# Slack for steps off the recurrence in an order planner, in a two-layer encoder kernel

## The chip, the cores and the metric

One Trainium2 chip, one of its cores. The metric is the device time of one execution of the whole kernel in microseconds (us), lower is better. A core has a matrix engine (PE, with its weight loads PEld), a vector engine (DVE), an activation engine (ACT), GpSimd (POOL) and a queue of transfers (SP); each runs its own list of instructions strictly in the order in which the program gives them.

## The reference

Two layers over 2048 frames of 1024 channels, all in float32:

```python
c_act = silu(c)
for i in range(2):
    shift, scale, gate = split(c_act @ ada_w[i] + ada_b[i])
    h = rmsnorm(x, norm_g[i]) * (1 + scale) + shift
    out = rglru_block(h, ...) if i == 0 else gated_deltanet_block(h, ...)
    x = x + gate * out
return rmsnorm(x, final_g)

# rglru_block: xb, zg = h @ in_w; causal conv of width 4 on xb; two gates, each a
#   product of 8 blocks of 128x128; a linear scan over time; y * silu(zg) @ out_w
# gated_deltanet_block, 8 heads of 128: q, k, v, z = h @ in_w; causal conv of width 4 and
#   silu on q, k, v; q and k to unit length; then by head, chunk after chunk,
#   step: v_new = u_c - w_c @ state;  o_c = q_c @ state + attn_c @ v_new
#         state = state * e_c + k_c^T @ v_new
#   o * rsqrt(mean(o^2) + eps) * onorm_g * silu(z) @ out_w
```

## The kernel before

A float32 product is made as three matmuls of a rounded type: each operand is split into a high part `hi` (a cast, on ACT) and a low part `lo` (`raw - hi`, on GpSimd for weights), and hi*hi, hi*lo, lo*hi are summed. The weights come in panels of 128 columns (512 KB): `panels_thread` loads one into a buffer `raw`, casts it to `whi` (L640) and subtracts to `wlo` (L646). There are two `raw` buffers, and the rows of the adaLN weights (`araw`, L402) and the output weights (`oraw`, L892) use the same two. `products` (L664) then issues 24 matmuls of 128x512 for one panel and one half of the tokens, into a PSUM bank `mm`. The 2048 frames are taken in two halves of 1024 (`u`), each in two parts of 512 (`i`): layer 1 is `in1` 0 and 1, then its output product `out1`, layer 2 `in2` 0 and 1, then `out2`.

In layer 2, `conv2_thread` copies the bank to `xe` on ACT (L726), which frees the bank, and convolves it on DVE (`xf`, L714), to a `kt`, `qt` or `vt` tile. By head and part, off the state's recurrence:

- `key_thread` loads the row of decays to all partitions (`ec`, L1117), masks it on GpSimd (L1119), takes its exponential on ACT (L1123) and makes the block matrix `ac`.
- `norm_q_thread` turns q by 32x32 blocks on DVE (`tokens_of`, `tb`), writes it to DRAM (`q_d`, L1223), reads it back as `pq` (L1197) and sums its squares on ACT (`junkq`, L1203); GpSimd makes `rq` of it.
- `value_thread` does the same with v (`v_d`, `vn`, L1235), and scales it on ACT (L1239).
- `outputs_thread` makes the scale `ro` on GpSimd (L1482), applies it on ACT (`oo`, L1487), turns it and writes `o_d`.
- `inverses_thread` and `levels_thread` invert the block (long runs of small DVE operations, `ttmp` and `tblk`, L1285 and L1288).

`recurrence_thread` then runs the chunks one after the other: `pp` on PE from the state (L1405), `zt` on DVE (L1414), `py` on PE (L1422), `yt` on ACT (L1428), `pS` on PE (L1434), `state` on DVE (L1447). The matmuls of the next heads' panels are issued between these steps.

Nothing of this order is written by hand. Each `..._thread` is a Python generator, and the class `Weave` is a planner that runs while the program is built: a thread yields what it needs next, `Weave.run` always takes the thread that can start first by its own account of time, and its instructions are written down at that point. The order in which they are written is the order of each engine's list. What a thread yields is `(engine, duration)` or `(engine, duration, lag)`, where `lag` is how long after the end a follower may start (0.2 us for POOL where none is given); `("sp", bytes)`, a transfer; `("none", t)`, a pause; a named event; or a set of buffers (`slots`), of which `put` frees one. The times in these tuples decide the order alone: on the chip an instruction waits for semaphores and nothing else.

The `hf` tag is a pair of 256 KB buffers that the turns share: `xb` of the input (`turn_thread`), `tb`, `pq` and `ob`.

Of the kernel before, what the change touches and what calls it, by code (L numbers as in the profile page):

```python
# [30 lines left out]
TURN = 2  # L31
BLK = 2
KTN, QTN = 6, 5
EPS = 1e-6


# [102 lines left out]
def trunk_kernel(ctx, tc, x, c, ada_w, ada_b, ada_c, norm_c, final_g, w1, cw1, cb1, gate_w, gate_b, lam, ow1,  # L139
                 w2, wab, cw2, a_log, dt_bias, onorm, ow2, out):  # L140
    nc = tc.nc
    act, dve, pool, pe, sp = nc.scalar, nc.vector, nc.gpsimd, nc.tensor, nc.sync
# [88 lines left out]
    def ev(*key):  # L231
        return events.setdefault(key, Event())

    def put(tag, token):
        w.put(slots[tag], token)
# [4 lines left out]
    def rsqrt(out, ssq, mul, n):  # L240
        pool.tensor_scalar(ssq, ssq, mul, EPS, ALU.mult, ALU.add)
        pool.tensor_tensor(out, ssq, mhalf[:, 0:n], ALU.pow)
# [196 lines left out]
        w.set(ev("gates"))  # L439


    def scale_thread(xt, done):
        stok = yield slots["ss"]
        rtok = yield slots["rs"]
        ttok = yield slots["tt"]
        yield "act", 1.04
        junk = tile_([P, D], "tt", "sqj", BF16)
        ss = tile_([P, 1], "ss", "ss")
        act.activation(junk, xt, AF.Square, accum_out=ss)
        put("tt", ttok)  # L450
        yield "pool", 0.75
        rs = tile_([P, 1], "rs", "rs")
        rsqrt(rs, ss, 1.0 / D, 1)
        put("ss", stok)
        yield "dve", STT
        dve.tensor_scalar(xt, xt, rs, None, ALU.mult)
        put("rs", rtok)
        w.set(done)
# [36 lines left out]
            put(tag, tok)  # L495

    def turn_thread(key, t_d, xt, tok, ttok, b):
        yield from scale_thread(xt, ev("scaled", key, b))
        for d in range(2):
            htok = yield slots["hf"]  # L500
            yield "dve", EV
            tb = tile_([P, KT * 2, 32], "hf", "xb")
            dve.transpose(out=tb, in_=xt[:, d * TC:(d + 1) * TC].rearrange("p (a j) -> p a j", j=32))
            if d == 1:
                put("b4", tok)
            dst = t_d[4 * d:4 * d + 4, :, b * P:(b + 1) * P].rearrange("k (r i) (c j) -> c i (k r) j", i=32, j=32)
            for c_ in range(4):
                yield "sp", 64 * KB, c_ == 3
                sp.dma_start(out=dst[c_], in_=tb[32 * c_:32 * c_ + 32])
            put("hf", htok)  # L510
        put("turn", ttok)
        w.set(ev("turned", key, b))
# [95 lines left out]
    def panels_thread():  # L608
        yield ev("small")
        ahead = []  # L610
        for name, panels, _ in plans:
            for m, p in enumerate(panels):

                if m == 2 and name == ("in2", 0):
                    yield ev("owt", 1, 1)
                    yield ev("gates")
                if m == 0 and name == ("in1", 0):
                    for q in panels[0:2]:
                        ahead.append((yield from panel_load(name, q)))
                    w.set(ev("firstpanels"))  # L620
                if m in (2, len(panels) - 1) or m < 2 and name != ("in1", 0):
                    if name == ("in1", 0):
                        yield ev("adaissue", 3)
                    ahead.append((yield from panel_load(name, p)))
                htok = yield slots["whi"]
                ltok = yield slots["wlo"]
                if not ahead:
                    ahead.append((yield from panel_load(name, p)))
                raw, rtok = ahead.pop(0)
                lo = tile_([P, KT, P], "wlo", "wlo", F32R)  # L630
                if name[1] > 0:

                    kept = yield ev("kept", p)
                    yield "sp", 512 * KB, False
                    sp.dma_start(out=f(lo), in_=kept)
                    w.spawn(arrive_thread(ev("lo", name, p)), 0)
                yield ev("raw", name, p)
                yield "act", 0.95
                hi = tile_([P, KT, P], "whi", "whi", F32R)
                act.copy(hi, raw)  # L640
                if name[1] > 0:
                    put("raw", rtok)
                    yield ev("lo", name, p)
                else:
                    yield "pool", 2.3
                    pool.tensor_tensor(lo, raw, f(hi), ALU.subtract)  # L646
                    put("raw", rtok)
                    w.spawn(keep_thread(p, lo), 5)
                w.set(ev("w", name, p), (hi, lo, htok, ltok))
# [460 lines left out]
    def key_thread(u, h, i):  # L1110
# [4 lines left out]
        yield "sp", 256 * KB  # L1115
        ec = tile_([P, TB, P], "ec", "ec")
        sp.dma_start(out=ec, in_=g_d[h:h + 1, i * TC:(i + 1) * TC].to_broadcast([P, TC]))  # L1117
        yield "pool", 0.7
        pool.affine_select(out=ec, in_=ec, compare_op=ALU.is_ge, fill=-1e30, base=0, pattern=[[0, TB], [1, P]],  # L1119
                           channel_multiplier=-1)  # L1120
        for b in range(TB):
# [69 lines left out]
    def norm_q_thread(u, h, i):  # L1191
        qt, qtok = yield ev("q", u, h, i)
        q_d = yield from tokens_of(qt, "q_d")
        htok = yield slots["hf"]
        yield "sp", 256 * KB
        pq = tile_([P, TB, P], "hf", "pq")
        sp.dma_start(out=pq, in_=q_d.rearrange("b p d -> p b d"))  # L1197
        stok = yield slots["ssq"]
        ss = tile_([P, TB], "ssq", "ssq")
        for b in range(TB):  # L1200
            yield "act", 0.295, 0.0
            junk = tile_([P, P], "junk", "junkq", BF16)
            act.activation(junk, pq[:, b, :], AF.Square, accum_out=ss[:, b:b + 1])  # L1203
        put("hf", htok)
        rtok = yield slots["rq"]
        yield "pool", 1.5
        rq = tile_([P, TB], "rq", "rq")
        rsqrt(rq, ss, 1.0, TB)
        pool.tensor_scalar(rq, rq, P ** -0.5, None, ALU.mult)
        put("ssq", stok)  # L1210
        w.set(ev("rq", u, h, i), (rq, rtok))

    def tokens_of(ap, name):

        htok = yield slots["hf"]
        yield "dve", EV
        tb = tile_([P, TB * 4, 32], "hf", "tb")
        dve.transpose(out=tb, in_=ap.rearrange("p (a i) -> p a i", i=32))
        t_d = dram.tile([TB, P, P], F32, tag=name, name=name, bufs=4)
        dst = t_d.rearrange("b (c j) (r i) -> r j (b c) i", j=32, i=32)  # L1220
        for r in range(4):
            yield "sp", 64 * KB, r == 3
            sp.dma_start(out=dst[r], in_=tb[32 * r:32 * r + 32])  # L1223
        put("hf", htok)
        return t_d

    def value_thread(u, h, i):

        vt, vtok = yield ev("v", u, h, i)
        v_d = yield from tokens_of(vt, "v_d")  # L1230
        put("vt", vtok)
        ntk = yield slots["vn"]
        yield "sp", 256 * KB
        vn = tile_([P, TB, P], "vn", "vn")
        sp.dma_start(out=vn, in_=v_d.rearrange("b p d -> p b d"))  # L1235
        nk, ntok = (yield ev("key", u, h, i))[-2:]
        for b in range(TB):
            yield "act", 0.255, 0.0
            act.activation(vn[:, b, :], vn[:, b, :], AF.Copy, scale=nk[:, b:b + 1])  # L1239
        put("nk", ntok)  # L1240
        w.set(ev("vn", u, h, i), (vn, ntk))
# [232 lines left out]
    def outputs_thread(u, h, i, oo, otok, so, sotok):  # L1474
        for b in range(TB):
            yield ev("o", u, h, i * TB + b)
        rq, qtok = yield ev("rq", u, h, i)
        rtok = yield slots["ro"]
        yield "pool", 1.4
        ro = tile_([P, TB], "ro", "ro")  # L1480
        rsqrt(ro, so, 1.0 / P, TB)
        pool.tensor_tensor(ro, ro, rq, ALU.mult)  # L1482
        put("so", sotok)
        put("rq", qtok)
        for b in range(TB):
            yield "act", 0.255, 0.0 if b < TB - 1 else 0.27
            act.activation(oo[:, b, :], oo[:, b, :], AF.Copy, scale=ro[:, b:b + 1])  # L1487
        put("ro", rtok)

        htok = yield slots["hf"]  # L1490
        yield "dve", EV
        ob = tile_([P, TB * 4, 32], "hf", "ob")
        dve.transpose(out=ob, in_=oo.rearrange("p b (e i) -> p (b e) i", i=32))
        put("oo", otok)
        if u == NU - 1:
            w.set(ev("oput", h, i))
        b0 = (u * NTC + i) * TB
        dst = o_d[b0:b0 + TB, :, h].rearrange("b (e i) g j -> g i (b e) j", i=32)
        for g in range(4):
            yield "sp", 128 * KB, g == 3  # L1500
            sp.dma_start(out=dst[g], in_=ob[32 * g:32 * g + 32])
        put("hf", htok)
        w.set(ev("od", u, h, i))

# [164 lines left out]
    with tc.manual_schedule():  # L1669
# [3 lines left out]
        in1, in2 = [("in1", u) for u in range(NU)], [("in2", u) for u in range(NU)]  # L1673
# [107 lines left out]
```

## Time and profile before

| what | value |
|---|---|
| median of 3 runs | 1968.5 us (1966.23 to 1977.2) |
| the profiled execution, time | 1969.04 us |
| its span, first to last instruction | 1967.3 us |
| PE busy | 1849.4 us (94%) |
| DVE, ACT, POOL busy | 1469.3, 1050.9, 640.5 us |
| mean granted PE clock | 0.983 |

The profile gives for each instruction its start, its duration and, where its engine stood idle ahead of it, how long and what ended the wait (`<-`). A group or a wait is named by the tile that is written and the line of the kernel.

### The profile page before, as it was taken

How to read it: one execution, taken by the hardware profiler on the slowest of the kernel's cores; microseconds unless marked ns; L12 is line 12 of the kernel's file. 1: busy time of each engine (PE TensorE's matmuls, PEld its weight loads, DVE VectorE, ACT ScalarE, POOL GpSimd, SP SyncE). 2: the span in 40 equal slices, each digit the busy share in tenths (PEclk: the TensorE clock that was granted, in tenths of full speed). 3: DMA queues.
4: the chain of work that ended last, by engine and by line, in shares of the span. 5: the costliest groups of instructions: out<-in, count | busy, mean ns of one | idle time of the engine just before them, and what ended most of it. 6: DMA issues, size and time to landing. Idle time of an engine off the chain costs nothing.

```text
span 1967.3 us, 31401 instructions
## 1 busy us (share of the span) xinstructions
PE 1849.4 (94%) x10286; PEld 1501.0 (76%) x10286; DVE 1469.3 (75%) x3271; ACT 1050.9 (53%) x2585; POOL 640.5 (33%) x1116
## 2 busy tenths in 40 slices
PE   6999898999999999998889999998999999999998
PEld 3777677887777777786777777777888888878887
DVE  6898888887645577878787888667777778876653
ACT  3667577766121345564655666465566566654221
POOL 3354532223000235344434543232332334410101
PEclk8999999999999999999999999999999999999999
DMA  8476736555688334566774447365356455576751
GB/s 315 115 211 190 236 131 192 159 175 163 215 219 226 134 110 138 129 158 159 180 176 116 125 118 198 99 185 137 99 146 164 121 142 146 137 221 204 240 168 65
DMA packets 511724, 322.77 MB, mean 164 GB/s; under 512 B 371268, under 2 KB 439236, under 8 KB 511560
## 3 DMA queue, kind: packets, MB, share of 16 engines
q1 hardware_dynamic: 511560, 320.77, 57.8%
q8 instruction: 81, 1.33, 0.3%
q14 instruction: 83, 0.68, 0.1%
HBM read 219.93 MB, written 100.73 MB: 163 GB/s over the span
## 4 chain that ended last, share of the span: by engine, by line
PE 52%; DVE 17%; DMA 12%; ACT 6%; issue 6%; SPq 4%; POOL 3%; DVEq 0%; POOLq 0%; ACTq 0%
PE mm L664 28%; PE mmo L664 12%; DVE xf L714 3%; PE pg L803 2%; DMA raw<-in_w 2%; DVE tblk L1288 2%; DMA pq<-q_d 2%; DVE ttmp L1285 2%; SPq L1223 1%; DMA ada<-in_ada_w 1%; PE pkk L1165 1%; PE pS L1434 1%; ACT junkq L1203 1%; PE py L1422 1%; PE pp L1405 1%
## 5 line engine op out<-in xcount | busy, mean ns | idle before, releaser
L714 DVE SCALAR_TENSOR_TENSOR xf<-xe,cw_s,xf 128x512 f32<-128x512 f32 x288 | 237.6, 829 | 28.5 <-POOL xf L993 23.8
L646 POOL TENSOR_TENSOR wlo<-raw,whi 128x1024 fp32r<-128x1024 f32 x48 | 119.6, 2492 | 129.1 <-ACT whi L640 125.7
L640 ACT CAST whi<-raw 128x1024 fp32r<-128x1024 f32 x96 | 100.6, 1047 | 79.2 <-DMA raw<-in_w 55.0
L1285 DVE TENSOR_TENSOR ttmp<-blk,tblk 128x60 f32<-128x60 f32 (+24 forms) x496 | 114.4, 231 | 25.7 <-DMA blk<-blk_d 12.8
L1288 DVE TENSOR_TENSOR tblk<-tblk,ttmp 128x60 f32<-128x60 f32 (+24 forms) x496 | 123.6, 249 | 10.0 <-POOL tblk L1279 0.2
L664 PE MATMUL mm<-hh_('in2', 1)_12236,whi 128*128 128x512 f32 x256 | 105.7, 413 | 2.6 <-ACT xe L726 2.6
L664 PE MATMUL mm<-hh_('in2', 0)_5231,whi 128*128 128x512 f32 x256 | 104.8, 409 | 3.5 <-ACT xe L726 3.5
L664 PE MATMUL mm<-hh_('in2', 0)_5454,whi 128*128 128x512 f32 x256 | 104.3, 408 | 2.0 <-ACT xe L726 2.0
L664 PE MATMUL mm<-hl_('in2', 0)_5455,whi 128*128 128x512 f32 x256 | 105.2, 411 | 0.0
L664 PE MATMUL mmo<-oh,yl 128*128 128x512 f32 x256 | 101.7, 397 | 3.4 <-DVE yl L925 3.4
L664 PE MATMUL mm<-hh_('in2', 0)_5231,wlo 128*128 128x512 f32 x256 | 104.8, 409 | 0.0
L664 PE MATMUL mm<-hh_('in2', 1)_12236,wlo 128*128 128x512 f32 x256 | 104.6, 409 | 0.0
L664 PE MATMUL mm<-hl_('in2', 0)_5232,whi 128*128 128x512 f32 x256 | 104.5, 408 | 0.0
L664 PE MATMUL mm<-hh_('in2', 1)_12412,wlo 128*128 128x512 f32 x256 | 104.5, 408 | 0.0
L664 PE MATMUL mm<-hl_('in2', 1)_12237,whi 128*128 128x512 f32 x256 | 104.3, 407 | 0.0
L664 PE MATMUL mm<-hh_('in2', 0)_5454,wlo 128*128 128x512 f32 x256 | 104.1, 407 | 0.0
L664 PE MATMUL mmo<-oh,yh 128*128 128x512 f32 x256 | 101.3, 396 | 2.8 <-ACT yh L921 2.8
L664 PE MATMUL mm<-hl_('in2', 1)_12413,whi 128*128 128x512 f32 x256 | 103.2, 403 | 0.0
L664 PE MATMUL mm<-hh_('in2', 1)_12412,whi 128*128 128x512 f32 x256 | 103.1, 403 | 0.0
L664 PE MATMUL mmo<-oh,oh 128*128 128x512 f32 (+1 forms) x264 | 102.7, 389 | 0.2 <-DVE tz L1021 0.2
L664 PE MATMUL mmo<-ol,oh 128*128 128x512 f32 (+1 forms) x264 | 102.8, 390 | 0.0
L664 PE MATMUL mmo<-ol,yh 128*128 128x512 f32 x256 | 101.3, 396 | 1.4 <-DVE ol L905 1.4
(331 smaller groups left out, 5633.1 us busy)
## 6 DMA issues: line engine op xcount, KB each, us to landing
raw<-in_w SPq DMA_DIRECT2D x96, 512.0 KB, 4.2
araw<-in_ada_w SPq DMA_DIRECT2D x32, 512.0 KB, 4.5
xt<-x_d SPq DMA_DIRECT2D x32, 512.0 KB, 4.4
xt_d<-xb SPq DMA_DIRECT2D x192, 64.0 KB, 2.6
xk<-xt_d SPq DMA_DIRECT2D x24, 512.0 KB, 6.0
xt<-in_x SPq DMA_DIRECT2D x16, 512.0 KB, 5.1
ada<-in_ada_w SPq DMA_DIRECT2D x16, 512.0 KB, 7.7
y_d<-tz SPq DMA_DIRECT2D x32, 256.0 KB, 3.7
```

What stands on the lines that cost most here:

```text
L640: act.copy(hi, raw)
L646: pool.tensor_tensor(lo, raw, f(hi), ALU.subtract)
L664: pe.matmul(pt, lhsT=lhs[a][:, k, :], rhs=rhs[b][:, k, :], start=(k == 0 and n == 0), stop=(k == KT - 1 and n == 2))
L714: dve.scalar_tensor_tensor(xf, xe[:, 1 + j:1 + j + TC], wc[:, j:j + 1], xf, ALU.mult, ALU.add)
L803: pe.matmul(pg, lhsT=a[:, g, :], rhs=b, start=(q == 0), stop=(q == 2))
L1165: pe.matmul(pkk[:, b, :], lhsT=kc, rhs=kc, start=True, stop=True)
L1203: act.activation(junk, pq[:, b, :], AF.Square, accum_out=ss[:, b:b + 1])
L1223: sp.dma_start(out=dst[r], in_=tb[32 * r:32 * r + 32])
L1285: dve.tensor_tensor(tmp, blk[:, j, j + 1:32].unsqueeze(2).to_broadcast([P, r, c_]), t[:, j, 0:c_].unsqueeze(1).to_broadcast([P, r, c_]), A ...
L1288: dve.tensor_tensor(t[:, j + 1:32, 0:c_], t[:, j + 1:32, 0:c_], tmp, ALU.subtract)
L1405: pe.matmul(pp[:, 0, :], lhsT=kc, rhs=S_, start=True, stop=True)
L1422: pe.matmul(py, lhsT=rm[:, b, :], rhs=zt, start=True, stop=True)
```

## The change

A constant `MARGIN = 2.4` is added, and the planner is told of more time at certain steps: a pause, or a longer lag. No instruction, tile or transfer is added or removed but for loads of ACT's function tables, whose number follows from the order (33 at lines 813, 826 and 853 before, 35 now). Lines of the new file are up to 9 higher than those of the old one.

```diff
+MARGIN = 2.4
-    def scale_thread(xt, done):
+    def scale_thread(xt, done, late=False):
...
-        yield "pool", 0.75
+        yield "pool", 0.75, MARGIN / 2 if late else 0.2
...  turn_thread: scale_thread(..., True); and behind the writes of xt_d
+            yield "none", MARGIN / 2
             put("hf", htok)
...  panels_thread
                 yield ev("raw", name, p)
+                if name[0] == "in2":
+                    yield "none", MARGIN / 2
                 yield "act", 0.95
...  key_thread, behind the load of ec
-        yield "pool", 0.7
+        yield "none", MARGIN / 2
+        yield "pool", 0.7, MARGIN / 2
         pool.affine_select(out=ec, ...)
...  norm_q_thread, behind the load of pq
+        yield "none", MARGIN
         stok = yield slots["ssq"]
...  tokens_of, behind the writes of q_d or v_d
+        yield "none", MARGIN / 2
         put("hf", htok)
...  value_thread, behind the load of vn
+        yield "none", MARGIN
         nk, ntok = (yield ev("key", u, h, i))[-2:]
...  outputs_thread
-        yield "pool", 1.4
+        yield "pool", 1.4, MARGIN / 2
...  outputs_thread, behind the writes of o_d
+        yield "none", MARGIN / 2
         put("hf", htok)
```

What that does to the order, at two places. The first is ACT's list in layer 2, first half, near its end: `junkq` reads `pq`, and `t` and `yt` are steps of the recurrence. Before:

```order
L1428 ACTIVATE yt<-py 128x128
L1461 ACTIVATE t_12032<-pp,eg 128x128
L1203 ACTIVATE junkq,ssq<-pq 128x128 x4
L1019 ACTIVATE tz<-mm 128x512
L1471 ACTIVATE junko,so<-oo,rq 128x128
L1203 ACTIVATE junkq,ssq<-pq 128x128 x3
L1461 ACTIVATE t_12101<-pp,eg 128x128
L1203 ACTIVATE junkq,ssq<-pq 128x128
L1428 ACTIVATE yt<-py 128x128
L1487 ACTIVATE oo<-oo,ro 128x128 x3
```

The same two groups of `junkq` after the change (L1209 is the old L1203, L1436 the old L1428, L1469 the old L1461):

```order
L1469 ACTIVATE t_12099<-pp,eg 128x128
L1436 ACTIVATE yt<-py 128x128
L1209 ACTIVATE junkq,ssq<-pq 128x128 x4
L1479 ACTIVATE junko,so<-oo,rq 128x128
L1495 ACTIVATE oo<-oo,ro 128x128 x3
L1469 ACTIVATE t_12164<-pp,eg 128x128
L1436 ACTIVATE yt<-py 128x128
L1209 ACTIVATE junkq,ssq<-pq 128x128 x4
L1495 ACTIVATE oo<-oo,ro 128x128
```

Both groups now stand right behind a `yt`; before, the second stood ahead of the next `t` and `yt`. In all of layer 2, the median number of 128x512 products on PE that stand in the program between a transfer and its reader goes from 4 to 7 for `pq`, from 2.5 to 7 for `vn`, from 10 to 11 for `raw`; between GpSimd's step and its reader from 1.5 to 3 for `ec` and from 5.5 to 10 for `ro`. The steps `yt` stand 3.5 products later on average than before.

The second place is SP's list in layer 1, second half, from the load of the third panel (`raw1`) to that of the fourth (`raw9`); `y_d` is written with a result, `yf` read, `gw` and `wlo` are other loads. Before:

```order
L604 DMA raw1_2412<-in_w1 128x1024
L845 DMA y_d_69<-tz_2243 128x512
L863 DMA gw_2506<-in_gate_w 128x256
L635 DMA wlo_2549<-wlo_d1x1_624 128x1024
L402 DMA araw_2575<-in_ada_w 128x1024
L892 DMA oraw_2577<-in_ow1 128x1024
L845 DMA y_d_69<-tz_2436 128x512
L917 DMA yf_2616<-y_d_69 128x8x128
L917 DMA yf_2679<-y_d_69 128x8x128
L845 DMA y_d_69<-tz_2503 128x512
L892 DMA oraw_2698<-in_ow1 128x1024
L604 DMA raw9_2700<-in_w1 128x1024
```

After:

```order
L606 DMA raw1_2487<-in_w1 128x1024
L896 DMA oraw_2506<-in_ow1 128x1024
L637 DMA wlo_2569<-wlo_d1x1_624 128x1024
L849 DMA y_d_69<-tz_2369 128x512
L403 DMA araw_2586<-in_ada_w 128x1024
L896 DMA oraw_2588<-in_ow1 128x1024
L921 DMA yf_2609<-y_d_69 128x8x128
L606 DMA raw9_2670<-in_w1 128x1024
```

The same three users of the two `raw` buffers stand between the two panels, in another order, and fewer other transfers. The load of `raw9` stood 8 products ahead of the panel's first product in the program, and now stands 35 ahead. In the first half of layer 1 another panel goes the other way: the load of `raw5` stood 37 products ahead of its panel's first product, and now 9.

More of the change, by code (lines that the diff above doesn't have):

```diff
@@ L497, in turn_thread @@
     def turn_thread(key, t_d, xt, tok, ttok, b):
-        yield from scale_thread(xt, ev("scaled", key, b))
+        yield from scale_thread(xt, ev("scaled", key, b), True)
         for d in range(2):
```

## Prediction

> **What bounds the kernel now.** I read the page first, for the engine that limits the whole, then its chain.
>
> ```profile
> span 1967.3 us, 31401 instructions
> ...
> PE 1849.4 (94%) x10286; PEld 1501.0 (76%) x10286; DVE 1469.3 (75%) x3271; ACT 1050.9 (53%) x2585; POOL 640.5 (33%) x1116
> ...
> PE 52%; DVE 17%; DMA 12%; ACT 6%; issue 6%; SPq 4%; POOL 3%; DVEq 0%; POOLq 0%; ACTq 0%
> ```
>
> PE works for 94% of the span, so the most that any order can win is its idle time, 1967.3 - 1849.4 = 118 us. The chain of work is only half PE's: it leaves PE often, for short pieces on DVE, in transfers and on ACT. Next I cut the span into stages and took PE's busy time in each.
>
> ```profile
> 0.00:50.00 50.00, 30.27 (x101) 18.26 (x102) 34.26 (x74) 18.59 (x31) 18.34 (x33) 0.88 0.80 310
> 50.00:690.00 640.00, 612.59 (x2625) 489.18 (x2625) 480.56 (x705) 347.23 (x491) 188.19 (x185) 0.98 0.60 182
> 690.00:1780.00 1090.00, 1026.70 (x6715) 844.54 (x6714) 849.77 (x2356) 633.23 (x1940) 412.35 (x844) 0.99 0.57 148
> 1780.00:1967.30 187.30, 179.87 (x852) 149.05 (x849) 104.74 (x138) 51.80 (x124) 21.60 (x55) 0.99 0.52 160
> ```
>
> The first number behind the length is PE's busy time. Idle are 19.7 us at the start, 27.4 us in layer 1 with its output, 63.3 us in layer 2 and 7.4 us at the end. Nearly all of the edit lies in layer 2, so I asked there whom PE waited for, longest first:
>
> ```profile
> PE pS L1434 <- ACT yt L1428: 12.3, 13, 1.7
> PE mm L664 <- ACT xe L726: 8.1, 5, 2.6
> PE pp L1405 <- DVE state L1447: 7.3, 6, 1.8
> PE pk L1130 <- DVE tblk L1288: 6.1, 3, 2.3
> PE py L1422 <- DVE zt L1414: 4.4, 5, 1.6
> PE pk L1130 <- DVE kt L1010: 4.0, 4, 1.4
> ```
>
> (Total us, times, longest.) Two rows end with ACT, 12.3 + 8.1 = 20.4 us; ACT is busy for 633 of 1090 us there, so it was late for another reason than load. What ACT itself waited for, of the steps that the change gives slack:
>
> ```profile
> ACT whi L640 <- DMA raw<-in_w: 30.9, 24, 3.0
> ...
> ACT junkq L1203 <- DMA pq<-q_d: 23.2, 20, 3.0
> ...
> ACT ec L1123 <- POOL ec L1119: 21.6, 17, 2.7
> ...
> ACT vn L1239 <- DMA vn<-v_d: 20.7, 13, 3.1
> ...
> ACT oo L1487 <- POOL ro L1482: 10.4, 10, 2.1
> ```
>
> Together 106.8 us in 84 waits. An engine takes its list in order, so whatever stands behind such a wait, a `yt` or an `xe`, waits too. One place shows the whole path:
>
> ```profile
> 1206.95 0.31 ACT L1203 ACTIVATE junkq<-pq 128x128 bf16<-128x128 f32 x1 [1.76 <-DMA pq<-q_d]
> ...
> 1208.13 0.35 ACT L1461 ACTIVATE t<-pp,eg 128x128 f32<-128x128 f32 x1
> ...
> 1208.67 0.26 ACT L1428 ACTIVATE yt<-py 128x128 f32<-128x128 f32 x1
> ```
>
> ```profile
> 1208.98 0.49 PE L1434 MATMUL pS<-yt,kd 128*128 128x128 f32 x2 [1.35 <-ACT yt L1428]
> ```
>
> ACT stands 1.76 us for `pq`, the four sums and `t` follow, then `yt`; PE stands 1.35 us for that `yt`. So the case for the change is real: reads of late transfers delay the recurrence through ACT's list.
>
> **The change part by part.** No work is added, so each term is a wait that goes, stays or comes.
>
> *Reads on ACT in layer 2 (raw, pq, ec, vn, ro).* A product costs about 9.54 / 42 = 0.227 us:
>
> ```profile
> 1166.62 9.54 PE mm L664 x42
> ```
>
> By the medians given with the order, `pq` gets 3 products more between transfer and reader (0.7 us), `vn` 4.5 (1.0), `raw` 1 (0.2), `ec` 1.5 (0.3), `ro` 4.5 (1.0). Taken off each of their waits: 20 x 0.7 = 14, 13 x 1.0 = 13, 24 x 0.2 = 5, 17 x 0.3 = 5, and for `ro` all 10, since its mean wait, 10.4 / 10, is no longer than what is taken off. That is 47 of 106.8 us, 44%. PE's waits on ACT should fall by the same share: 0.44 x 20.4 = 9.0 us. Bounds: all 20.4 us go; or none, if the waits are ones that the planned distance doesn't govern (first rival).
>
> *The clock.* After such a gap PE is not at once at full speed:
>
> ```profile
> 907.63 0.50 PE L664 MATMUL mm<-hh_('in2', 0)_5231,whi 128*128 128x512 f32 x1 [1.97 <-ACT xe L726]
> ```
>
> ```profile
> 907.50:911.50 4.00, 3.87 (x10) 3.09 (x11) 2.10 (x6) 2.36 (x5) 3.75 (x9) 0.57 0.68 168
> 911.50:915.00 3.50, 3.50 (x21) 3.03 (x20) 3.50 (x4) 0.30 (x1) 3.50 (x4) 1.00 0.25 38
> ```
>
> Behind a gap of 1.97 us the granted clock is 0.57 for 4 us and 1.00 again after that: (1 - 0.57) x 4.0 = 1.7 us lost beside the gap. Of the five waits for `xe` I count one such pair as going with its gap: 1.7 us. Bounds 0 to 5 x 1.7 = 8.5.
>
> The Trainium skill ("TensorE: Matmul & The Clock Gate", section "What's actually happening") says that the clock falls to half after at least one idle window of about 3.4 us. This trace shows it fall after 1.97 us. By the page's figure a gap of that length would cost no clock, and the sum would be 1.7 us smaller.
>
> *The hole at 308 us in layer 1.* The largest gap of PE behind the start is this:
>
> ```profile
> 304.80 0.33 SPq L604 DMA_DIRECT2D raw<-in_w  x1
> ```
>
> ```profile
> 312.25 1.05 ACT L640 CAST whi<-raw 128x1024 fp32r<-128x1024 f32 x1 [0.21 <-DMA raw<-in_w]
> ```
>
> ```profile
> 313.35 0.80 PE L664 MATMUL mm<-hh_('in1', 1)_1902,whi 128*128 128x512 f32 x1 [5.35 <-ACT whi L640]
> ```
>
> ```profile
> 313.30:317.50 4.20, 4.15 (x10) 3.28 (x11) 3.35 (x4) 4.18 (x6) 0.94 (x2) 0.50 0.73 268
> ```
>
> A panel is issued at 304.80, lands 7.4 us later, is cast by 313.30, and PE has been out of work for 5.35 us; then the clock is 0.50 for 4.2 us, 2.1 us more. This is the load of `raw9`, which the new order puts 35 instead of 8 products ahead of its use, 27 x 0.227 = 6.1 us earlier. That covers the 5.35 us, and the whole hole, 7.5 us, can go. Against that stands `raw5`, now only 9 products = 2.0 us ahead of its use:
>
> ```profile
> raw<-in_w SPq DMA_DIRECT2D x96, 512.0 KB, 4.2
> ```
>
> With 4.2 us to land and 1.05 us for the cast it would be late by 4.2 + 1.05 - 2.0 = 3.2 us, if PE keeps to the plan there; before, the trace shows no gap at that panel. I take a gain of 7.5 - 3.5 = 4.0 us for layer 1, the 3.5 being that lateness and a little for other panels; bounds are the full 7.5, and a loss of 3.2 + 2.1 = 5.3 if another panel takes over the hole with its clock and the gain at `raw9` is lost.
>
> *Buffers held longer (`hf`) and GpSimd's lag in the turns.* On the chip a buffer is freed when its transfer has landed, whatever the planner says, so this only moves `tb`, `xb` and `ob` later in DVE's list. What hides it: those results are needed a head later. The `yt` of the plan stand 3.5 products later, 0.8 us, once and not per head; with something for the two more table loads, which lie on ACT beside PE's products, I charge 1.0 us. Bounds: 0 (all hidden) and 3.4, two waits as long as the longest on `yt`, 1.7 us.
>
> Sum: -9.0 - 1.7 - 4.0 + 1.0 = -13.7 us. The profiled execution took 1969.04 us, 1.7 above its span and 0.5 above the median of the runs; 1968.5 - 13.7 = 1954.8, so 1955 us.
>
> **The rivals.**
>
> *The waits stay.* The planner pauses from when it believes a transfer lands. On the chip the transfer itself is often issued late, because SP waits for the write of the same data:
>
> ```profile
> SPq L1197 <- DMA q_d<-tb: 27.6, 28, 3.7
> ```
>
> ```profile
> 1202.18 0.31 ACT L1203 ACTIVATE junkq<-pq 128x128 bf16<-128x128 f32 x1 [1.17 <-DMA pq<-q_d]
> ```
>
> The reader at 1202.18 stands 8 products behind its transfer in the old order, more than the new median of 7, and still waited 1.17 us. If distance governs only a third of the waits, the first term is 0.33 x 9.0 = 3 us, the clock term 0, and the sum -3 - 4 + 1 = -6: 1962 us, within the 0.5% (9.8 us) that a measurement of this kernel can just tell from no change. For it speaks this row; against it, that 18 readers of `pq` and 21 of `vn` stood 4 products or fewer behind their transfers, and 14 and 10 do now.
>
> *GpSimd's long subtraction falls on the recurrence more often.* The change moves `whi`, and with it `wlo`, in layer 2.
>
> ```profile
> 1200.72 2.41 POOL L646 TENSOR_TENSOR wlo<-raw,whi 128x1024 fp32r<-128x1024 f32 x1 [11.21 <-ACT whi L640]
> ```
>
> ```profile
> 1200.64 0.23 DVE L1285 TENSOR_TENSOR ttmp<-blk,tblk 128x72 f32<-128x72 f32 x1
> 1200.91 2.30 DVE L1288 TENSOR_TENSOR tblk<-tblk,ttmp 128x72 f32<-128x72 f32 x1
> ```
>
> While `wlo` runs, a DVE operation of 0.23 us takes 2.30. All of DVE's list stands for 2.1 us, `state` and `zt` with it. There are 32 such subtractions in layer 2, all in its first half. PE's waits on `state` and `zt` are 7.3 + 4.4 = 11.7 us; at 1.7 us a hit (between the longest of the two rows, 1.8 and 1.6) that is 7 hits at most, and 25 of the 32 have yet to hit. To end slower by 0.5%, the change must lose 9.8 + 13.7 = 23.5 us, 14 more hits; I price the case at 1979 us. It decides if more than half of those 25 come to lie over a step of the recurrence, and nothing in the order aims them there.
>
> The Trainium skill ("GPSIMD Engine Reference", section "1. Specifications") says that GpSimd's interfaces to SBUF are shared with VectorE, with contention for DVE operations that have two SBUF inputs; the trace agrees, 2.30 against 0.23 us. By that rule any order that doesn't know of it, this one too, gains or loses by chance.
>
> *The layer-1 order is re-dealt for the worse.* `raw5` and others with 9 products or fewer take over the hole of 308 us: +5.3 in place of -4.0, the layer-2 gain stays: -9.0 - 1.7 + 5.3 + 1.0 = -4.4, 1964 us.
>
> **How the numbers follow.** Chances: the forecast 0.57; the waits stay 0.19; layer 1 for the worse 0.11; GpSimd on the recurrence 0.13. The forecast's own range, from the bounds of its terms, is 1968.5 - 20.4 - 8.5 - 7.5 + 0 = 1932 at most far, and with half of the second bounds 1940, up to 1959. The whole range reaches over the two small gains to a little above no change, and cuts off about a tenth at either side: 1938 to 1974. Faster by over 0.5%, below 1958.7: the forecast, 0.57, less 0.02 at its upper end, and a little of the second case: 0.57. Slower, above 1978.3: most of the GpSimd case, 0.10, and 0.02 for what I haven't named: 0.12. Between: 0.31.
>
> **What would show it.** PE's wait of `pS` on `yt` in layer 2 should fall from 12.3 to about 7 us and that on `xe` from 8.1 to 5; ACT's waits on `pq` from 23.2 to 9 and on `vn` from 20.7 to 8, on `raw` hardly; PE's idle time of 63.3 us in layer 2 to some 53. The gap of 5.35 us on `whi` in layer 1 should be gone. I am wrong if ACT's waits fall and PE's don't, since then DVE was the next to be late; if they don't fall at all; or if gaps on `state` and `zt` grow beyond 11.7 us.

## The result, and the profile after

| | median | range |
|---|---|---|
| before | 1967.6 us | 1966.2 to 1977.2 |
| changed | 1946.3 us | 1945.0 to 1949.0 |

The medians lie 21.4 us apart. The ratio on record is 0.9875 (95% interval 0.9853 to 0.9897), which is a little more, 24.6 us. The forecast was 1955 us, 13.7 us less than before.

The page of the changed kernel, its first lines and its chain of work:

```profile
span 1944.8 us, 31354 instructions
...
PE 1842.4 (95%) x10286; PEld 1505.7 (77%) x10286; DVE 1476.8 (76%) x3271; ACT 1048.0 (54%) x2587; POOL 652.2 (34%) x1116
...
PE 58%; DVE 19%; DMA 8%; ACT 6%; issue 4%; SPq 2%; POOL 2%; DVEq 0%; POOLq 0%; ACTq 0%
```

PE's idle time went from 117.9 to 1944.8 - 1842.4 = 102.4 us, 15.5 us of the 22.5 us by which the span fell. The other 7.0 us are PE's busy time for the same 10286 matmuls; the ends of matmuls are modelled, and I take that figure for no finding. The chain leaves PE less often: transfers and SP's queue have 10% of it, where they had 16%.

The stretches of the prediction, in the changed kernel (us; busy time and instructions of PE, PEld, DVE, ACT, POOL; granted clock; DMA share; GB/s):

```profile
50.00:690.00 640.00, 616.34 (x2644) 492.67 (x2643) 483.27 (x705) 348.95 (x494) 195.91 (x186) 0.98 0.61 182
690.00:1780.00 1090.00, 1038.40 (x6825) 865.54 (x6825) 869.40 (x2385) 641.13 (x1975) 422.19 (x849) 0.99 0.58 150
1780.00:1944.80 164.80, 157.82 (x721) 130.29 (x719) 89.68 (x109) 39.38 (x88) 16.72 (x49) 0.99 0.53 165
```

PE's idle time is 23.7 us in the second of the old stretches (it was 27.4) and 51.6 in layer 2's (63.3). In the same 1090 us PE now issues 6825 matmuls instead of 6715. Whom PE waits for there:

```profile
PE py L1430 <- DVE zt L1422: 10.3, 6, 2.8
PE pk L1135 <- DVE kt L1014: 8.7, 4, 4.7
PE pp L1413 <- DVE state L1455: 7.7, 7, 1.8
...
PE mm L668 <- ACT xe L730: 3.9, 4, 1.9
...
PE pS L1442 <- ACT yt L1436: 0.4, 1, 0.4
```

The two rows that end with ACT fell from 20.4 to 4.3 us. DVE leads the list now. And ACT's own waits in that stretch, of the steps with slack:

```profile
ACT whi L644 <- DMA raw<-in_w: 16.7, 12, 4.0
...
ACT oo L1495 <- POOL ro L1490: 7.9, 6, 1.7
...
ACT ec L1128 <- POOL ec L1124: 6.1, 5, 2.6
...
ACT vn L1247 <- DMA vn<-v_d: 2.1, 1, 2.1
...
ACT junkq L1209 <- DMA pq<-q_d: 1.1, 1, 1.1
```

One wait for `pq` is left, of 1.1 us; the five together fell from 106.8 to 33.9 us.

### The profile page after: what moved, and what is told of

Its sections match the earlier page's. It is cut to its first block, busy times and chain, and to the rows that moved or that the text cites. A ratio compares the mean times of both kernels' runs of the same rounds, so it can differ in the third digit from the quotient of the medians.

```text
span 1944.8 us, 31354 instructions
## 1 busy us (share of the span) xinstructions
PE 1842.4 (95%) x10286; PEld 1505.7 (77%) x10286; DVE 1476.8 (76%) x3271; ACT 1048.0 (54%) x2587; POOL 652.2 (34%) x1116
## 4 chain that ended last, share of the span: by engine, by line
PE 58%; DVE 19%; DMA 8%; ACT 6%; issue 4%; SPq 2%; POOL 2%; DVEq 0%; POOLq 0%; ACTq 0%
PE mm L668 30%; PE mmo L668 15%; DVE xf L718 3%; DVE tblk L1296 2%; DVE ttmp L1293 2%; PE py L1430 1%; PE pg L807 1%; PE pp L1413 1%; PE pS L1443 1%; DMA raw<-in_w 1%; PE pS L1442 1%; PE pp L1414 1%; DMA ada<-in_ada_w 1%; DVE xf L756 1%; PE pqk L1258 1%
## 5 line engine op out<-in xcount | busy, mean ns | idle before, releaser
L718 DVE SCALAR_TENSOR_TENSOR xf<-xe,cw_s,xf 128x512 f32<-128x512 f32 x288 | 231.4, 806 | 28.1 <-POOL xf L997 24.1
L644 ACT CAST whi<-raw 128x1024 fp32r<-128x1024 f32 x96 | 100.0, 1042 | 53.9 <-DMA raw<-in_w 48.3
L668 PE MATMUL mm<-hh_('in2', 1)_12379,whi 128*128 128x512 f32 x256 | 104.8, 409 | 2.6 <-ACT xe L730 2.6
L668 PE MATMUL mm<-hh_('in2', 0)_5437,whi 128*128 128x512 f32 x256 | 105.3, 411 | 1.0 <-ACT xe L730 1.0
L668 PE MATMUL mm<-hl_('in2', 0)_5438,whi 128*128 128x512 f32 x256 | 105.5, 412 | 0.0
L668 PE MATMUL mm<-hh_('in2', 0)_5342,whi 128*128 128x512 f32 x256 | 103.8, 405 | 1.5 <-DVE tz L1025 1.5
L668 PE MATMUL mm<-hh_('in2', 0)_5437,wlo 128*128 128x512 f32 x256 | 104.5, 408 | 0.0
L668 PE MATMUL mm<-hh_('in2', 1)_12201,whi 128*128 128x512 f32 x256 | 104.1, 407 | 0.3 <-ACT xe L730 0.3
L668 PE MATMUL mm<-hh_('in2', 1)_12379,wlo 128*128 128x512 f32 x256 | 104.3, 407 | 0.0
L668 PE MATMUL mm<-hh_('in2', 0)_5342,wlo 128*128 128x512 f32 x256 | 103.9, 406 | 0.0
L668 PE MATMUL mm<-hh_('in2', 1)_12201,wlo 128*128 128x512 f32 x256 | 103.8, 406 | 0.0
L668 PE MATMUL mm<-hl_('in2', 1)_12380,whi 128*128 128x512 f32 x256 | 103.6, 405 | 0.0
```

Source lines behind the costliest of these rows:

```text
L668: pe.matmul(pt, lhsT=lhs[a][:, k, :], rhs=rhs[b][:, k, :], start=(k == 0 and n == 0), stop=(k == KT - 1 and n == 2))
L718: dve.scalar_tensor_tensor(xf, xe[:, 1 + j:1 + j + TC], wc[:, j:j + 1], xf, ALU.mult, ALU.add)
```

## The experiments

The edits fall into three groups: the slack at reads (`raw`, `pq`, `ec` with its mask, `vn`, `ro`), the later return of `hf` in the turns of q, v and the output, and the same with GpSimd's lag in `turn_thread`. The expectations name their theories by letters. Three stood at first: A, the prediction's, that the reads carry the gain and the rest is hidden; B, that any new deal of the order would have done as well; C, that the loads of layer 1's panels and the `raw` buffers carry it. D, that the return of `hf` carries it, was put up only after `hold`.

All ratios are to the kernel before on the same chip; its medians there lay between 1967.6 and 1972.2 us. To see where the time lies I also cut every trace at the same products on PE: layer 1 with its output from the first product of `in1` to the first of `in2`, and layer 2 from there to the last product of `out2`. These lengths are worked out from the traces' rows of products, one profiled execution of each kernel:

| kernel | ratio (95% interval) | median, us | layer 1, us | layer 2, us |
|---|---|---|---|---|
| before | 1 | 1967.6 | 636.9 | 1286.8 |
| changed | 0.9875 (0.9853 to 0.9897) | 1946.3 | 632.2 | 1268.9 |
| reads | 0.9944 (0.9924 to 0.9963) | 1957.9 | 639.4 | 1269.8 |
| rawonly | 1.0045 (1.0031 to 1.0059) | 1978.2 | 646.8 | 1284.6 |
| hold | 0.9868 (0.9844 to 0.9891) | 1943.2 | 626.5 | 1273.9 |
| turn | 0.9960 (0.9945 to 0.9975) | 1963.3 | 626.5 | 1289.3 |
| hf2 | 0.9929 (0.9914 to 0.9944) | 1958.5 | 637.2 | 1273.3 |
| noraw | 0.9877 (0.9848 to 0.9906) | 1947.0 | 628.1 | 1274.9 |
| m48 | 0.9927 (0.9903 to 0.9952) | 1955.5 | 632.5 | 1279.9 |
| early_src | 0.9984 (0.9969 to 0.9999) | 1969.1 | 640.3 | 1285.5 |
| own_pq | 1.0003 (0.9986 to 1.0019) | 1972.3 | 636.6 | 1287.9 |
| pause | 1.0026 (1.0003 to 1.0048) | 1975.0 | 637.0 | 1291.7 |
| deal1 | 1.0016 (1.0000 to 1.0031) | 1975.5 | 634.5 | 1294.0 |
| deal2 | 1.0015 (1.0002 to 1.0029) | 1976.0 | 646.5 | 1284.5 |

One profile of `early_src` and of `own_pq`, which keep the old order to the letter, differs from before by up to 3.4 us in a column, and a profiled execution lies up to 2.9 us from its kernel's median. Smaller differences are not read.

**`reads`: the slack at `pq`, `ec`, `vn` and `ro` alone.** The changed kernel without these edits:

```diff
-        yield from scale_thread(xt, ev("scaled", key, b), True)
+        yield from scale_thread(xt, ev("scaled", key, b))
-            yield "none", MARGIN / 2      # ahead of put("hf", htok), 3 places
-                if name[0] == "in2":
-                    yield "none", MARGIN / 2
```

> Slack only at the four reads of layer 2 (pq, vn, ec with GpSimd's mask, ro); none at raw, at the shared hf buffers or in the turns. Theory A (late small transfers hold ACT's list, and with it yt and xe): most of the gain, 12 to 18 us below before, PE's wait of pS on yt near 1 us from 12.3. Theory B (any other deal of the order does as well, the old one was a bad draw): between -10 and +10 us, no link to those waits. Theory C (the gain is the panels' loads in layer 1 and the raw buffers): 0 to -3 us.

0.9944, about 11 us. In layer 2 the profiled execution shows 17.0 us less; it lies 2.7 us below this kernel's median. PE's longest waits for the recurrence over the whole span of this kernel, then ACT's on the small reads:

```profile
PE pp L1409 <- DVE state L1451: 8.9, 9, 2.2
...
PE pS L1438 <- ACT yt L1432: 5.3, 6, 2.1
...
PE py L1426 <- DVE zt L1418: 4.9, 5, 1.6
```

```profile
ACT oo L1491 <- POOL ro L1486: 8.2, 6, 2.4
...
ACT junkq L1206 <- DMA pq<-q_d: 6.2, 4, 2.9
...
ACT ec L1125 <- POOL ec L1121: 4.0, 3, 2.4
```

These waits of ACT's fall, and `pS` waits 5.3 us for `yt` where it waited 12.3; no wait for `xe` is left in layer 2. The path that the prediction drew exists, and moved by itself it is worth about the 10.7 us of the prediction's first two terms, less than the 12 to 18 us that A expected here, as the wait on `yt` is not near 1 us either. ACT's waits for `raw` in layer 2 rose at the same time, from 30.9 to 49.8 us, and PE's waits on ACT fell all the same.

**`rawonly`: the slack at layer 2's raw panels alone.**

```diff
+                if name[0] == "in2":
+                    yield "none", MARGIN / 2
```

> Slack only at the raw panels of layer 2. Theory A: -1 to -4 us, since ACT waits 30.9 us for raw but PE's wait on yt is mostly behind pq and vn. Theory B: between -10 and +10 us. Theory C: -5 us or more.

1.0045: slower by about 9 us. All of it lies in layer 1, 646.8 against 636.9 us, although the slack is at layer 2's panels. They share the two `raw` buffers with layer 1's late panels, so the planner deals those anew too. A and C had both expected a gain here; this piece by itself is a loss.

**`hold`: `hf` and GpSimd's lag alone, no slack at a read.** These are the lines taken out in `reads`, but for the raw panels', added to the kernel before:

```diff
+        yield from scale_thread(xt, ev("scaled", key, b), True)
+            yield "none", MARGIN / 2      # ahead of put("hf", htok), 3 places
```

> Slack only where the hf buffers are given back and in GpSimd's step of the turned input, so layer 1 is as in the changed kernel up to the first panels of layer 2. Theory A: layer 1 with its output ends some 4.5 us earlier, layer 2 as before: -3 to -6 us in all. Theory B: between -10 and +10 us. Theory C: -8 us or more.

0.9868, about 26 us: as much as the whole change, where A had expected 3 to 6. Layer 1 is 10.4 us shorter and layer 2 12.9, so C, which looked to layer 1 and `raw`, has at most half of it. PE's waits in this kernel, then ACT's:

```profile
PE pp L1408 <- DVE state L1450: 11.0, 8, 2.2
PE pS L1437 <- ACT yt L1431: 8.7, 9, 2.0
...
PE mm L666 <- ACT xe L728: 5.6, 2, 3.9
```

```profile
ACT ec L1125 <- POOL ec L1121: 21.5, 19, 2.8
...
ACT oo L1490 <- POOL ro L1485: 13.9, 16, 4.5
ACT junkq L1205 <- DMA pq<-q_d: 13.6, 11, 2.5
...
ACT vn L1242 <- DMA vn<-v_d: 10.7, 9, 2.0
```

Without any slack at a read, `pq` falls from 23.2 to 13.6 us and `vn` from 20.7 to 10.7, while `ec`, which uses no `hf`, stays. So the return of `hf` moves the reads as well. That the gain needs no slack at the reads is shown, and not that the reads' waits have no part in it: PE's gaps behind ACT in layer 2 (690 to 1780 us) fall from 24.1 to 15.8 us. Which rows make up the 26 us is not shown, since `yt` still costs 8.7 us.

**`turn` and `hf2`: the two halves of `hold`.** `turn` has only the edits of `turn_thread` (the lag of `scale_thread` and one `hf`), `hf2` only the two pauses behind the writes of `q_d`, `v_d` and of `o_d`.

> Slack only in the turns of the input (GpSimd's step of the turned rows late, hf given back late behind the writes of xt_d), which lie in layer 1, its output product and the first half of layer 2. Theory D: the part of the 26 us gain that came ahead of the second half of layer 2 and its input turns, -8 to -14 us. Theory B: between -15 and +10 us.

> Slack only where hf is given back behind the writes of q_d, v_d and o_d in layer 2; layer 1 is that of before. Theory D: the rest of the 26 us, -8 to -16 us, all of it in layer 2, with DVE's wait ahead of tb near 1 us from 8.8. Theory B: between -15 and +10 us.

0.9960 and 0.9929, about 8 and 14 us. By the table they lie apart: `turn` takes 10.4 us off layer 1 and nothing off layer 2, `hf2` 13.5 us off layer 2 and nothing off layer 1. Their sum is `hold` in each column, within the 3 us. Both came within the range that D gave, and DVE has no wait ahead of `tb` left in `hf2`; the range that B gave here, -15 to +10 us, holds both as well, so these two runs don't part the theories. Whom DVE waited for in layer 1 (50 to 690 us), before and then in `turn`:

```profile
DVE xt L456 <- POOL rs L242: 15.4, 8, 6.7
...
DVE xb L503 <- DMA xt_d<-xb: 12.6, 8, 3.4
```

```profile
DVE xt L457 <- POOL rs L243: 9.0, 7, 3.1
...
DVE xb L504 <- DMA xt_d<-xb: 5.6, 2, 4.0
```

These are the two waits that the edit of `turn_thread` is aimed at: DVE stood for a scale of GpSimd's and for a buffer, and its list waited behind. And the first row of PE's waits in layer 1 of `turn`, longest first:

```profile
PE pg L805 <- DVE xl L799: 8.8, 9, 2.1
```

The hole on `whi` is gone here too. It stands, with 5.3 to 5.8 us, in `reads`, `rawonly`, `hf2`, `early_src`, `own_pq` and `pause`, none of which has the edit of `turn_thread`. So this edit is what moved the load of `raw9`. It is not the only order that does: `deal1` has no hole on `whi` either.

**`early_src`: the reads early, the order unchanged.** `pq` and `vn` are loaded from rows of the layer's input, written long ago, so that no write of the same data stands ahead of them; the norms of q and the values are then of other data.

```diff
-        sp.dma_start(out=pq, in_=q_d.rearrange("b p d -> p b d"))
+        sp.dma_start(out=pq, in_=x1_d[i * TC:(i + 1) * TC, h * P:(h + 1) * P].rearrange("(b p) d -> p b d", p=P))
...  and the same for vn
```

> The old order, unchanged, but pq and vn are loaded from rows of x1 that were written long before, so the loads don't wait for the writes of q_d and v_d (norms of q and the values are those of other data). Theory A: ACT's 44 us of waits on pq and vn shrink to under 15, PE's wait of pS on yt from 12.3 to about 6, time 5 to 12 us below before. Theories B and C: within 3 us of before.

0.9984: next to nothing. ACT's waits and PE's in this kernel:

```profile
ACT junkq L1203 <- DMA pq<-x_d: 14.8, 16, 2.9
...
ACT vn L1239 <- DMA vn<-x_d: 13.5, 9, 3.2
```

```profile
PE pS L1434 <- ACT yt L1428: 9.9, 10, 1.4
...
PE mm L664 <- ACT xe L726: 8.6, 5, 2.6
```

The two reads wait 28.3 us instead of 43.9, where A expected under 15, and A's gain of 5 to 12 us did not come. ACT's waits for `raw` rose from 30.9 to 39.3 us, so the five rows together fell by 7% only. PE's waits on ACT fell from 20.4 to 18.5 us, 9%, and the time by 0.16%, 3 us. The write ahead of the read is not the main delay: a read that need not wait for it is late nearly as often (25 waits for 33), and moving the reader, as in `reads`, takes most of the wait away (6.2 us left for `pq`). What holds these reads up was not measured.

**`own_pq`: a buffer of its own for `pq`, the old order.** The planner does not know of it; `kt` gives up one of its six buffers for the room.

```diff
-        pq = tile_([P, TB, P], "hf", "pq")
+        pq = tile_([P, TB, P], "q_pq", "pq")
+    tags["q_pq"] = ("l2", 1)     # behind the planner's own count of buffers
+    tags["kt"] = ("l2", 5)
```

> The old order, instruction by instruction, but pq has a buffer of its own, so that the two hf buffers serve the turns alone; the room comes from one of six kt buffers. Theory D (DVE's turns wait on the chip for hf buffers whose writes have not landed): DVE's wait ahead of tb from 8.8 to under 4 us and 3 to 10 us below before. Theory G (what counts is where the planner puts the turns in DVE's list, not the buffer): within 4 us of before, whatever the wait does. If waits for the missing kt buffer grow, it tells nothing.

1.0003, no change. DVE's wait for a `tb` fell from the 8.8 us of four rows before to this one row (the second is PE's):

```profile
DVE tb L1220 <- DMA q_d<-tb: 1.7, 1, 1.7
```

```profile
PE pS L1436 <- ACT yt L1430: 13.0, 14, 2.2
```

No row shows DVE waiting for the missing `kt` buffer. So the shortage of `hf` on the chip, as far as `tb` shows it, is not what `hold` cured, and D fails in the form that its expectation gave it. DVE's wait ahead of `xb` for the writes of `xt_d`, 12.6 us before, is 12.4 here: for layer 1 this run shows nothing. A third `hf` for all users was not tried.

**`pause`: as much slack in the same threads, in another place.** 1.2 us ahead of the request for `hf` in the turns of q, v and the output, in place of 1.2 us ahead of its return:

```diff
+        yield "none", 1.2
         htok = yield slots["hf"]
```

> The kernel before with one pause of 1.2 us in the plan ahead of each turn of q, v and the output in layer 2, before it asks for an hf buffer; nothing is given back later and no transfer is waited for there. Theory G (what counts is that the turns stand later in DVE's list against the recurrence, for whatever reason): -8 to -16 us, as the slack behind the writes alone (-14). Theory I (the slack has to stand where the plan is too early, behind a transfer; the same pause elsewhere buys nothing): within 5 us of before, DVE's wait ahead of tb still above 4 us.

1.0026, slightly slower. ACT's waits in this kernel:

```profile
ACT junkq L1203 <- DMA pq<-q_d: 25.3, 19, 5.0
...
ACT ec L1123 <- POOL ec L1119: 24.1, 15, 5.0
...
ACT vn L1240 <- DMA vn<-v_d: 6.2, 6, 1.6
```

Later turns alone don't help: theory G is out, and theory I held. The pause has to stand behind the write. There it does two things in the plan: it keeps the next user of the buffer off, and it puts off the thread's own next step, the load of `pq` or `vn`. No run parts the two. SP's waits for the writes of `q_d` and `v_d` ahead of these loads bear on the second: 27.6 + 26.3 = 53.9 us in layer 2 before, 14.5 + 15.3 = 29.8 in `hf2`, 40.6 + 24.6 = 65.2 here. But in `early_src` nearly all of them are gone, 5.5 us, and the time hardly moved, so they are not the cost by themselves.

**`deal1` and `deal2`: two random orders.** Every duration that the planner hears is multiplied by a random factor:

```diff
+                w = (w[0], w[1] * self.rng.uniform(0.95, 1.05), *w[2:])
```

> The kernel before, but the planner multiplies each engine duration by a random factor from 0.95 to 1.05 (seed 1): the order is dealt anew in both layers without any slack. Theory B (any new deal does it, the old order was a bad draw): 10 to 25 us below before. Theory D (it is the slack where hf is given back: DVE's turns waited for buffers whose writes had not landed): within 8 us of before, DVE's waits ahead of tb and xb near 24 us as before.

> As the first random deal, with seed 2. Theory B: 10 to 25 us below before. Theory D: within 8 us of before. The two seeds together tell how far a deal alone moves the time.

1.0016 and 1.0015. Two deals are few, but both moved the time by 3 us, and to the wrong side. `reads`, `turn` and `hf2` each gained more than twice that. So a lucky deal is a poor account of the gain as a whole. By the columns it is less clear: `deal2` made layer 1 9.7 us longer, and `deal1` made layer 2 7.2 us longer. A deal alone can move one layer nearly as far as `turn` moved layer 1, 10.4 us, though here it did so to the wrong side; that luck has a part in that figure is not excluded.

**`noraw`: the changed kernel without the slack at the raw panels.**

```diff
-                if name[0] == "in2":
-                    yield "none", MARGIN / 2
```

> The changed kernel without the slack at the raw panels of layer 2, so slack at hf, the turns and the four reads. Theory E (the raw slack costs some 9 us, as it did alone, and hides the gain of the reads): 30 to 37 us below before, 8 or more faster than the changed kernel. Theory F (hf and the reads cure the same waits, so the gains don't add): -20 to -28 us, as the changed kernel.

0.9877 against the changed kernel's 0.9875: in the whole, this piece costs and brings nothing, although alone it cost 9 us. Theory F held and E failed. By the columns the piece does both: with it layer 1 is 4.1 us longer, layer 2 6.0 us shorter. And `hf` and the four reads together, without it, take 11.9 us off layer 2, no more than `hf2` (13.5) or `reads` (17.0) alone. Pieces of such a change don't add.

**`m48`: `MARGIN = 4.8`.**

> The changed kernel with MARGIN 4.8 in place of 2.4. Theory D and A together (slack beyond what transfers are late buys nothing and delays the parts of the next heads): -15 to -25 us, no better than the changed kernel. Theory H (still more slack, still fewer waits): -26 us or lower.

0.9927. More slack is worse than 2.4, though faster than none. Its `pS` waits as little for `yt` as the changed kernel's, and PE waits for DVE, longest first over the whole span:

```profile
PE py L1430 <- DVE zt L1422: 9.6, 8, 1.8
PE pp L1413 <- DVE state L1455: 8.4, 7, 2.3
...
PE pS L1442 <- ACT yt L1436: 0.4, 1, 0.4
```

The waits that the slack can reach are nearly used up at 2.4: PE's gaps behind ACT from 690 to 1780 us are 5.7 us in the changed kernel and 4.6 here, and the rest are DVE's. But these waits don't account for its being slower: from 690 to 1780 us PE's gaps of all kinds sum to 49.8 us here and to 51.0 in the changed kernel. What differs is the granted clock: 0.95 from 1000 to 1300 us where the changed kernel has 1.00, and 0.972 to 0.977 as the mean of each execution where it has 0.982 to 0.983. (1.00 - 0.95) x 300 is 15 us, an estimate; layer 2 is 11.0 us longer. Why the clock was lower there was not measured. No run beat the changed kernel beyond the intervals: `hold` and `noraw` stand level with it.

## Why the prediction was right, and where not

**Reads on ACT in layer 2, -9.0, and the clock, -1.7.** The first held as an effect of its own: `reads`, without the slack at `raw`, gave about 11 us. In the changed kernel the waits fell further than foreseen: `pS` on `yt` to 0.4 us instead of 7, `xe` to 3.9 (5), `pq` to 1.1 (9), `vn` to 2.1 (8), and `raw`, which should hardly have moved, to 16.7 from 30.9. `ro` missed the other way: all of its 10.4 us should have gone, and 7.9 stayed. PE's idle time in layer 2 came out at 51.6 us, where 53 was named. The clock term is not seen: the granted clock of that stretch is 0.99 before and after.

By the columns of the table the change took 4.7 us off layer 1, where 4.0 was forecast, and 17.9 off layer 2, where 9.7 was (9.0 + 1.7 - 1.0). So the forecast fell short in layer 2. The term that was mis-sized is the 44%: ACT's five waits fell by 68%, and PE's waits on ACT by 16.1 of 20.4 us, 79%. The largest misses are `ec` (15.5 us off instead of 5), `raw` (14.2 instead of 5) and `pq` (22.1 instead of 14).

The step that PE's waits on ACT fall by the same share as ACT's own does not hold with `raw` among the five. In `reads` the five fell by 36%, since `raw` rose to 49.8 us, and PE's waits on ACT by 74%. Over the four small reads alone it comes out in three kernels: they fell by 77% in the changed kernel (PE's waits by 79%), by 76% in `reads` (74%) and by 27% in `hold` (30%). It fits less in `noraw`, 75% (50%), and in `early_src`, 20% (9%).

**The hole at 308 us in layer 1, -4.0.** The hole went as forecast, and layer 1 is 4.7 us shorter. That the net is so close is in part luck: with the edit of `turn_thread` and no slack at `raw` layer 1 is 8.8 to 10.4 us shorter (`noraw`, `hold`, `turn`), more than the 7.5 us of the hole, and the slack at `raw` takes some of it back. The counter-term was not `raw5`, but a new hole near the end of the layer.

```profile
490.15 1.28 ACT L830 ACT_TABLE_LOAD   x1
...
492.09 1.28 ACT L783 ACT_TABLE_LOAD   x1
...
493.88 1.99 ACT L907 ACTIVATE oh<-oraw 128x1024 fp32r<-128x1024 f32 x2
...
494.98 0.80 PE L668 MATMUL mmo<-oh,yh 128*128 128x512 f32 x1 [4.85 <-ACT oh L907]
```

```profile
495.00:499.00 4.00, 2.05 (x4) 1.35 (x5) 4.00 (x4) 2.79 (x3) 2.79 (x2) 0.50 0.35 80
499.00:502.00 3.00, 3.00 (x9) 2.23 (x8) 2.78 (x3) 0.12 (x1) 0.05 (x1) 0.57 0.89 267
```

ACT, with two table loads in 3.7 us, casts `oh` late; PE stands 4.85 us, and the clock is at half for most of the 7 us that follow. In layer 1 PE waits 5.5 us for `oh` in all here, 5.2 in `rawonly` and 7.7 in `m48`, which have the slack at `raw`, and 1.1 to 1.2 in `noraw`, `hold` and `turn`, which don't. `noraw` differs from the changed kernel by this slack alone, and its layer 1 is 4.1 us shorter. So the slack at `raw` brings the hole; that the hole is the whole of the 4.1 us is argued from the rows.

**Buffers held longer (`hf`) and GpSimd's lag, +1.0.** This is the step that failed, in sign. I held that the chip frees a buffer when its transfer has landed, whatever the planner says, and that only DVE's list is moved, under cover. True, but the order is what the planner says. A buffer that it believes held 1.2 us longer puts the next `tb`, `xb` or `ob`, and the read that follows it, behind other work; whether the buffer or the read counts was not parted (`pause`). Alone this gave 8 us with the turns of `turn_thread`, and 14 with those of layer 2; the terms for the reads and for the hole in layer 1 are in part the same gain. In layer 2 `reads` shows 17.0 us, `hf2` 13.5, both groups without `raw` 11.9 (`noraw`), and the whole change 17.9: either alone does as much as both. Over the span from 50 us on, PE's gaps behind ACT sum to 34.9 us before, 18.2 in `reads`, 18.3 in `hold` and 14.4 in the changed kernel. The two groups take away much the same gaps, which leaves little for the second to win; the gaps behind DVE (56.4, 64.0, 50.2 and 59.5 us) are the rest.

**The rivals.** The waits did not stay. The re-deal of layer 1 came in part, as told. The rival of GpSimd's long subtraction came in part too: `state` and `zt` cost 18.0 us of gaps, beyond the 11.7 that I named as a sign of being wrong, and `kt` 8.7 instead of 4.0. Of the 18.0 us, 12.4 in eight waits lie beside a subtraction or up to 1 us behind one; before it was 8.3 us in five. Yet it didn't decide, because the gaps behind ACT fell by more. The longest of the waits on `kt`, in the changed kernel:

```profile
891.20 2.35 POOL L650 TENSOR_TENSOR wlo<-raw,whi 128x1024 fp32r<-128x1024 f32 x1 [1.52 <-ACT whi L644]
891.25 2.84 DVE L1014 SCALAR_TENSOR_TENSOR kt<-tt,xf 128x512 f32<-128x512 f32 x1
...
894.24 1.09 PE L1135 MATMUL pk<-ident,kt 128*128 128x128 f32 x4 [4.67 <-DVE kt L1014]
...
895.90 0.64 DVE L1014 SCALAR_TENSOR_TENSOR kt<-tt,xf 128x512 f32<-128x512 f32 x1
```

The same operation takes 2.84 us beside the subtraction and 0.64 without it. The Trainium skill ("GPSIMD Engine Reference", section "1. Specifications") has GpSimd and VectorE share their interfaces to SBUF, with contention for DVE operations with two SBUF inputs, as this one is; this trace agrees. In the second half of layer 2, which has no such subtraction, PE's waits from 1300 to 1700 us are these three in the changed kernel:

```profile
PE pk L1135 <- DVE ttmp L1293: 4.6, 1, 4.6
PE mm L668 <- ACT xe L730: 0.3, 1, 0.3
PE pp L1413 <- DVE state L1455: 0.2, 1, 0.2
```

5.1 us in 400. Of PE's 51.6 us of idle time in layer 2, 41.5 lie ahead of 1300 us (PE is busy for 287.24 us from 690 to 1000 and for 281.22 from 1000 to 1300).

**What stays open.** Why a later return of `hf` in the plan moves so much, as told under `pause`. Which of the moved steps makes up the whole gain of `hold`: `yt` and `xe` together (8.7 + 5.6 us, from 20.4) account for 6.1 us of it, and the two waits of DVE in layer 1 for some of the rest.

## What to carry to other kernels

Where a planner's account of time sets the order of in-order queues, tell it of more time behind each small transfer, and behind a buffer's return too: the chip needs no such pause, but the order of the next user follows from it. Measure the pieces apart and together before keeping or dropping one; here one cost 9 us alone and nothing in the whole, and two that gave 17 and 14 us in layer 2 gave 12 together. Once the waits of one engine are gone, look at which engine PE waits for next, and at the granted clock: twice the slack was slower here with as few gaps.

## What the runs showed that I had not expected

A gap on PE can cost well beyond its length: behind the 4.85 us at 495 us the granted clock was 0.50 for 4 us and 0.57 for the 3 us after, with a second gap of 1.95 us among them. And a DVE operation on 128x512 elements stretched from 0.64 to 2.84 us beside a GpSimd subtraction of 2.35 us, longer than the subtraction itself. I had counted such a hit at 1.7 us of PE's time; of the 4.67 us that PE stood here, 2.2 are this stretch, and PE had begun to wait 1.6 us before the subtraction began.
